# Strided attention on one core: another order of the first four loads

## The chip, the cores and the metric

The kernel runs on one core of a Trainium2 chip. The metric is the device time of one execution in microseconds (us), taken as the median of several runs; lower is better. Beside the times there is one execution recorded by the hardware profiler, with a trace of every instruction on the five engines (PE, the matrix engine; DVE, the vector engine; ACT, the scalar engine; POOL, the general engine; SP, which here only issues transfers) and of every packet that the 16 DMA engines moved.

## What is computed

Attention in which every query attends to only every 64th key, so 16 keys and 16 values for each of the 8 x 12 = 96 pairs of batch and head. The reference, cut to its core:

```python
# Q, K, V: float32, (batch, heads, seq, dim) = (8, 12, 1024, 64), stride = 64
for i in range(seq):
    attend_positions = np.arange(0, seq, stride)
    q = Q[:, :, i:i + 1, :]
    k = K[:, :, attend_positions, :]
    v = V[:, :, attend_positions, :]
    scores = np.einsum('bhqd,bhkd->bhqk', q, k) / np.sqrt(dim)
    weights = np.exp(scores - np.max(scores, axis=-1, keepdims=True))
    weights = weights / (np.sum(weights, axis=-1, keepdims=True) + 1e-10)
    result[:, :, i, :] = np.einsum('bhqk,bhkd->bhqd', weights, v)[:, :, 0, :]
```

Q is 25.17 MB, the result is as large, and the rows of K and V that are used are 0.39 MB each.

## The kernel before

**Tiling.** The 96 heads are cut into 24 groups of four (`NG = 24`, `HG = 4`). One group's queries are a block of 1 MiB (1.05 MB) that lands in one buffer `qn` as 128 partitions x 2048 floats. There are 18 such buffers (`BUFS = 18`), held two by two in the tiles `pair0` to `pair8`; a group's output is written back into the buffer that held its queries, and two groups are stored to HBM by one transfer of 2 MiB (the last two groups by one of 1 MiB each).

**Stages of a group.** `cast` turns the block to bf16 (tile `qb`; POOL alone at line 305, for the first three groups half on ACT at line 299 and half on POOL at line 301), `transpose` on DVE (`qt`, line 316), the products with the keys on PE (`sc`, line 324), the maximum and its subtraction on DVE (`top`, `low`), the exponential on ACT (`ex`, line 346), sum and reciprocal on DVE (`total`, `rec`), the multiplication on POOL (`wt_all`, line 358), a transpose on PE (`tp`), its spreading on ACT (`wb_all`, line 377), the products with the values on PE (`o`, line 385), and `evict` on ACT (line 403), which copies `o` into the query buffer. Then SP issues the store.

**Keys and values.** `load_rows` (line 235) fetches the 1536 used rows of K, and likewise of V, each row 256 bytes. `key_rows` casts the keys on ACT (line 263) and transposes them on DVE (line 264); `keys` (line 273) copies them into `k_t`, four copies on DVE for the even groups and four on ACT for the odd ones. `values` (line 287) places the values in `v_all`: eight small casts on POOL at once, the rest later on ACT and POOL.

**What sets the order.** Each engine has its instructions in the order in which the program was written out; an instruction that waits holds up everything behind it on its engine. On ACT this order begins: cast of the keys, half of query block 0, four copies of keys, half of query block 1, first exponential. On POOL: half of query block 0, the eight value casts, half of query block 1, half of query block 2, first `wt_all`. On DVE: transpose of the keys, four copies of keys, transpose of block 0.

All transfers are issued by SP on one hardware queue, from `_copy` (line 34, queries and outputs) or `load_rows` (line 236, keys and values), and each has its own semaphore. SP issues the first 20 loads back to back without waiting (K, query block 0, V, query blocks 1 to 17). From then on `queue` (line 454) sets its order: after every second group a store, and after the stores of groups 2-3, 4-5 and 6-7 two more query loads each (blocks 18 to 23). Block 18 goes into the buffer of group 0, block 19 into that of group 1, and so on, and SP waits until the store from that buffer has landed before it issues the load.

Of the kernel before, what the change touches and what calls it, by code (L numbers as in the profile page):

```python
# [18 lines left out]
def _ap_with(ap: bass.AP, new_ap, extra_offset: int = 0) -> bass.AP:  # L19
    return dataclasses.replace(  # L20
        ap, ap=[list(p) for p in new_ap], offset=ap.offset + extra_offset
    )


def _copy(nc, out: bass.AP, in_: bass.AP):

    sides = [
        mybir.BassSymbolicTensorAccessPattern(
            ap=side.ap, dtype=side.dtype, bass_ap=side,
            is_dma=True, for_custom_bir_dma=True,  # L30
        )
        for side in (in_, out)
    ]
    return nc.sync.add_instruction(  # L34
        mybir.InstDMACopy(
            name=nc.get_next_instruction_name(), engine=mybir.EngineType.SP,
            ins=sides[:1], outs=sides[1:], queue="qSPDynamicHW",
            mode="Copy",
        )
    )  # L40


class Program:
# [13 lines left out]
    def op(self, engine, fn, reads=(), writes=(), after=(), lane=None, gate=None, gates=(), times=1, looped=False, last=False):  # L57
        i = len(self.ops)
        deps, own = set(after), set()
        for k in reads:  # L60
            deps.add(self.writer.get(k))
            own.add(self.writer.get(k))
        for k in writes:
            deps.update(self.readers.get(k, ()))
            deps.add(self.writer.get(k))
            own.add(self.writer.get(k))
        deps.discard(None)
        for k in reads:
            self.readers.setdefault(k, []).append(i)
        for k in writes:  # L70
            self.writer[k], self.readers[k] = i, []
        self.ops.append(dict(
            engine=engine, fn=fn, lane=lane or engine, deps=deps, own=own,
            gate=gate, gates=gates, times=times, last=last, looped=looped,
        ))
        return i
# [92 lines left out]
def kernel(  # L169
# [21 lines left out]
    BUFS = 18  # L191
# [34 lines left out]
    def load(g):  # L226
        n = 32
        op("SP", lambda: _copy(
            nc, qn[g % BUFS],
            _ap_with(Q, [[HG * SD // n, n], [1, HG * SD // n]], g * HG * SD),  # L230
        ), writes=[f"qn{g % BUFS}{h}" for h in range(2)], lane=f"q{g % BUFS}")
# [3 lines left out]
    def load_rows(name, tile_, src, lane):  # L235
        op("SP", lambda: nc.sync.dma_start(tile_, _ap_with(src, kv_src)),
           writes=[name], lane=lane)

    load_rows("k_raw", k_raw, K, "k")
    load(0)  # L240
    load_rows("v_raw", v_raw, V, "v")
    for g in range(1, BUFS):
        load(g)

    op("POOL", lambda: nc.gpsimd.memset(identity, 0.0), writes=["identity"])
# [309 lines left out]
```

## Time and profile before

| | us |
|---|---|
| median of 3 runs | 128.17 |
| lowest and highest of them | 127.93 and 128.45 |
| the profiled execution, its own time | 127.63 |
| its span, first to last instruction | 125.8 |
| ACT busy in the span | 93.8 (75%) |
| DVE busy | 87.1 (69%) |
| POOL busy | 75.9 (60%) |
| PE busy | 58.1 (46%) |
| DMA queue busy, mean of 16 engines | 96.8% |

Read it from both ends. The shares of the compute engines are means over the span, and none of them works in the last fifth of it, so the shares say little of a single stage. The share of the DMA queue counts all 16 DMA engines. The page also draws the span as a line of 40 slices for each engine, a digit being the busy share in tenths; the time at the ends of these lines is what the argument below starts from. In tables by stretches of time, a packet's bytes are booked in the stretch in which it starts, so in short stretches the DMA share can be over 1.

### The profile page before, as it was taken

What the parts mean: (1) busy time and instruction counts of PE and PEld (TensorE: products, weight loads), DVE (VectorE), ACT (ScalarE), POOL (GpSimd) and SP (SyncE); (2) the same over time, 40 slices, a digit from 0 to 9 for tenths busy, and PEclk for the clock granted to TensorE, in tenths of its full rate; (3) what the DMA queues carried; (4) which work ended last, traced back from release to release, by engine and by line L of the source; (5) the groups of instructions that cost most, each with busy time, mean ns of one, the idle gap of its engine ahead of it and who ended that gap; (6) DMA issues with size and microseconds to landing.
All of it is one profiled execution on the core that took longest, in us unless ns stands there. A gap on an engine that the chain in (4) does not pass through costs nothing.

```text
span 125.8 us, 2084 instructions
## 1 busy us (share of the span) xinstructions
PE 58.1 (46%) x736; PEld 43.5 (35%) x736; DVE 87.1 (69%) x131; ACT 93.8 (75%) x109; POOL 75.9 (60%) x67
## 2 busy tenths in 40 slices
PE   0007672556489466665555565666656533000000
PEld 0006452445366444443443344444434321000000
DVE  3795879999979899999999999999966100000000
ACT  4266756999888999999999999999999965000000
POOL 5648589999998688889888888879233300000000
PEclk9999999998555999999999999999999975555555
DMA  1998989989899998999999999999999999999991
GB/s 41 425 406 385 490 365 479 448 385 479 365 479 437 406 469 354 422 422 479 417 391 458 422 385 432 464 406 424 417 422 422 427 427 437 427 432 417 406 424 65
DMA packets 6132, 51.15 MB, mean 406 GB/s; under 512 B 3696, under 2 KB 3696, under 8 KB 3696
## 3 DMA queue, kind: packets, MB, share of 16 engines
q1 hardware_dynamic: 6128, 51.12, 96.8%
q14 instruction: 4, 0.03, 0.1%
HBM read 25.95 MB, written 25.17 MB: 406 GB/s over the span
## 4 chain that ended last, share of the span: by engine, by line
ACT 51%; POOL 15%; DVE 7%; DMA 5%; PE 4%; issue 1%; SPq 1%; POOLq 0%
ACT pair L403 28%; ACT wb_all L377 16%; ACT ex L346 7%; POOL qb L305 6%; DMA v_raw<-in_V_dram 5%; POOL wt_all L358 4%; PE o L385 4%; POOL v_all L287 4%; DVE qt L316 3%; DVE total L351 1%; DVE top L338 1%; DVE rec L354 1%; POOL qb L301 1%; SPq L34 1%; DVE low L341 1%
## 5 line engine op out<-in xcount | busy, mean ns | idle before, releaser
L403 ACT COPY pair<-o 128x2048 f32<-128x2048 f32 x24 | 47.9, 1995 | 2.8 <-PE o L385 2.8
L305 POOL CAST qb<-pair 128x2048 bf16<-128x2048 f32 x21 | 39.7, 1892 | 1.5 <-DMA pair<-in_Q_dram 1.5
L385 PE MATMUL o<-v_all,wb_all 128*128 (+1 forms) x216 | 31.6, 295 | 8.2 <-ACT pair L403 8.2
L358 POOL TENSOR_TENSOR wt_all<-ex,rec 128x512 bf16<-128x512 f32 x24 | 25.4, 1058 | 15.4 <-DVE rec L354 15.1
L377 ACT ACTIVATE wb_all<-tp,sel 128x512 bf16<-128x512 bf16 x48 | 33.3, 810 | 0.7 <-PE tp L365 0.6
L316 DVE STREAM_TRANSPOSE qt<-qb 128x1024 int32<-128x1024 int32 x24 | 29.8, 1242 | 1.2 <-POOL qb L305 0.7
L385 PEld LDWEIGHTS o<-v_all,wb_all 128*128 128x128 bf16 x216 | 20.7, 105 | 14.9 <-issue 9.6
L324 PE MATMUL sc<-k_t,qt 128*128 x416 | 19.4, 200 | 12.9 <-DVE qt L316 12.8
L324 PEld LDWEIGHTS sc<-k_t,qt 128*128 128x128 bf16 x416 | 16.9, 103 | 17.5 <-issue 16.6
L365 PE MATMUL tp<-identity,wt_all 128*128 128x128 bf16 x104 | 11.1, 235 | 25.5 <-POOL wt_all L358 25.5
L346 ACT ACTIVATE ex<-low 128x512 f32<-128x512 f32 x24 | 18.3, 764 | 2.5 <-DVE low L341 2.5
L351 DVE TENSOR_REDUCE total<-ex 128x32 f32<-128x512 f32 x24 | 16.3, 678 | 3.9 <-ACT ex L346 3.9
L341 DVE TENSOR_TENSOR low<-sc,top 128x512 f32<-128x512 f32 x24 | 16.6, 691 | 0.8
L365 PEld LDWEIGHTS tp<-identity,wt_all 128*128 128x128 bf16 x104 | 6.4, 103 | 28.3 <-POOL wt_all L358 28.2
L338 DVE TENSOR_REDUCE top<-sc 128x32 f32<-128x512 f32 x24 | 15.2, 632 | 1.3 <-PE sc L324 1.3
L354 DVE RECIPROCAL rec<-total 128x32 f32<-128x32 f32 x24 | 8.5, 353 | 0.8
L287 POOL CAST v_all<-v_raw 32x128 bf16<-32x128 f32 (+1 forms) x12 | 5.2, 431 | 1.5 <-DMA v_raw<-in_V_dram 0.8
L299 ACT CAST qb<-pair 128x1024 bf16<-128x1024 f32 x3 | 3.1, 1045 | 3.1 <-DMA pair<-in_Q_dram 3.1
L301 POOL CAST qb<-pair 128x1024 bf16<-128x1024 f32 x3 | 3.1, 1039 | 3.3 <-DMA pair<-in_Q_dram 3.3
L259 POOL MEMSET v_all<- 128x3456 f32 x1 | 3.0, 2979 | 0.0
L287 ACT CAST v_all<-v_raw 32x640 bf16<-32x640 f32 x4 | 2.9, 722 | 0.0
L250 DVE MEMSET k_t<- 128x1664 uint32 x1 | 1.4, 1445 | 1.9 <-issue 1.9
(15 smaller groups left out, 9.6 us busy)
## 6 DMA issues: line engine op xcount, KB each, us to landing
pair<-in_Q_dram SPq DMA_DIRECT2D x24, 1024.0 KB, 15.0
out_dram<-pair SPq DMA_DIRECT2D x11, 2048.0 KB, 22.8
out_dram<-pair SPq DMA_DIRECT2D x2, 1024.0 KB, 18.7
k_raw<-in_K_dram SPq DMA_DIRECT2D x1, 384.0 KB, 3.9
v_raw<-in_V_dram SPq DMA_DIRECT2D x1, 384.0 KB, 6.8
```

Source lines behind the costliest of these rows:

```text
L305: op("POOL", lambda: nc.gpsimd.tensor_copy(out=b, in_=q), reads=[f"qn{g % BUFS}{h}" for h in range(2)] + apart, writes=[f"qb{g % 2}{h}" fo ...
L316: op("DVE", lambda: nc.vector.transpose(_ap_with(words, [words.ap[0], [1, 2], [D, 16], [2, 32]]), qb[g % 2].bitcast(I32),), reads=[f"qb{g ...
L324: r = nc.tensor.matmul(sc_ps[g % 2][:, 64 * i : 64 * i + 64], lhsT=_ap_with(qt[g % 2], [qt[g % 2].ap[0], [2, P]], extra_offset=2 * P * i + f),
L338: op("DVE", lambda: nc.vector.tensor_reduce(out=m, in_=s, op=ALU.max, axis=mybir.AxisListType.X,), reads=[f"sc{g % 2}"], writes=[f"top{g % ...
L341: op("DVE", lambda: nc.vector.tensor_tensor(out=low, in0=s, in1=m.unsqueeze(2).to_broadcast([P, 32, NK]), op=ALU.subtract,), reads=[f"sc{g ...
L346: op("ACT", lambda: nc.scalar.activation(out=ex[g % 2], in_=low, func=AF.Exp, bias=0.0, scale=scale,), reads=["low"], writes=[f"ex{g % 2}"])
L351: op("DVE", lambda: nc.vector.tensor_reduce(out=total[g % 2], in_=ex[g % 2], op=ALU.add, axis=mybir.AxisListType.X,), reads=[f"ex{g % 2}"] ...
L358: op("POOL", lambda: nc.gpsimd.tensor_tensor(out=wt[g % 2], in0=ex[g % 2], in1=rec[g % 2].unsqueeze(2).to_broadcast([P, 32, NK]), op=ALU.mult,
L365: r = nc.tensor.transpose(tp_ps[g % 2][:, 2 * c : 2 * c + 2].rearrange("p a b -> p (a b)"), wt[g % 2][:, 8 * c : 8 * c + 8].rearrange("p t ...
L377: op("ACT", lambda a=a: nc.scalar.activation(out=wb[g % 2][:, :, 64 * a : 64 * a + 64], in_=tp_ps[g % 2], func=AF.Copy, scale=sel[:, a : a ...
L385: r = nc.tensor.matmul(_ap_with(o_ps, [o_ps.ap[0], [128, 2], [256, 2], [1, D]], extra_offset=512 * c + D * u,), lhsT=wb[g % 2][:, 2 * c + ...
L403: op("ACT", lambda: nc.scalar.copy(to, o_ps.rearrange("p c (b x) -> p c b x", b=2)), reads=["o"], writes=[f"qn{g % BUFS}{n}" for n in rang ...
```

## The change

The first four loads are issued in another order: query block 0, K, query block 1, V, where it was K, query block 0, V, query block 1. Query blocks 2 to 17 follow as before. No instruction is added or removed, no size or wait of any engine is edited, and apart from these four transfers each engine has its instructions in the order it had.

```diff
@@ -236,10 +236,11 @@
         op("SP", lambda: nc.sync.dma_start(tile_, _ap_with(src, kv_src)),
            writes=[name], lane=lane)
 
+    load(0)
     load_rows("k_raw", k_raw, K, "k")
-    load(0)
+    load(1)
     load_rows("v_raw", v_raw, V, "v")
-    for g in range(1, BUFS):
+    for g in range(2, BUFS):
         load(g)
```

The place is the head of SP's stream. `pair0` is the tile that holds the buffers of query blocks 0 and 1, so both of its rows read alike; the first of them is block 0. Before:

```order
L236 DMA k_raw_71<-in_K_dram 128x12x64
L34 DMA pair0_62<-in_Q_dram 128x2048
L236 DMA v_raw_74<-in_V_dram 128x12x64
L34 DMA pair0_62<-in_Q_dram 128x2048
L34 DMA pair1_63<-in_Q_dram 128x2048 x2
```

After the change, the same place on SP:

```order
L34 DMA pair0_62<-in_Q_dram 128x2048
L236 DMA k_raw_71<-in_K_dram 128x12x64
L34 DMA pair0_62<-in_Q_dram 128x2048
L236 DMA v_raw_74<-in_V_dram 128x12x64
L34 DMA pair1_63<-in_Q_dram 128x2048 x2
```

K and V have each moved one place back, and each has now one query block more ahead of it in the queue; block 2 (the first of `pair1_63`) is where it was.

The engine that meets both of the moved loads early is POOL. With the change its stream reads as follows, row for row what it was (only the line numbers are one higher); `at_q0`, `at_q1`, `at_q2` and `at_v` are the semaphores of the loads of the query blocks 0 to 2 and of V:

```order
L302 CAST qb0_75<-pair0_62 128x1024 [waits at_q0]
L288 CAST v_all_82<-v_raw_74 32x2x64 [waits at_v,at_POOL]
L288 CAST v_all_82<-v_raw_74 32x2x64 [waits at_POOL] x7
L302 CAST qb1_76<-pair0_62 128x1024 [waits at_q1,at_POOL]
L144 UNCONDITIONAL_BRANCH
L302 CAST qb0_75<-pair1_63 128x1024 [waits at_q2,at_DVE,at_POOL]
```

Nothing moved here: the cast of block 1 still stands behind the eight casts of the values, although block 1 is now loaded ahead of them.

## The prediction

> **What bounds the kernel now.** I read the slices of the page first, then the end of the chain of waits, then the transfers.
>
> ```profile
> span 125.8 us, 2084 instructions
> DVE  3795879999979899999999999999966100000000
> ACT  4266756999888999999999999999999965000000
> DMA  1998989989899998999999999999999999999991
> 104.83 1.87 ACT pair L403
> 107.28 0.54 SPq L34 DMA_DIRECT2D out_dram<-pair  x1
> ```
>
> A slice is 3.1 us. The chain of waits ends with ACT's last eviction, at 104.83 + 1.87 = 106.7 us, and names ACT as half of the span; but that is where instructions end. The DMA line is full from the second slice to the last but one. The last store is issued at 107.28 us and the span runs 18.5 us longer, for a transfer of 1 MiB. How much was still queued is told by a table of stretches (columns: stretch, its length, busy time and count for PE, PEld, DVE, ACT, POOL, clock, DMA share, GB/s):
>
> ```profile
> 0.00:55.39 55.39, 29.03 (x359) 22.23 (x360) 47.59 (x69) 44.50 (x55) 44.85 (x45) 0.91 0.97 403
> 55.39:60.72 5.33, 3.45 (x52) 2.60 (x49) 5.19 (x10) 5.33 (x8) 4.23 (x4) 1.00 1.06 443
> 60.72:70.42 9.70, 5.98 (x84) 4.58 (x84) 9.53 (x15) 9.70 (x13) 8.14 (x6) 1.00 1.02 432
> 70.42:107.30 36.88, 19.66 (x245) 14.13 (x244) 24.80 (x41) 34.25 (x38) 18.71 (x14) 0.94 0.99 422
> 107.30:124.50 17.20, 0.00 (x0) 0.00 (x0) 0.00 (x0) 0.00 (x0) 0.00 (x0) 0.50 0.93 392
> ```
>
> After ACT's end the queue still moves 17.20 us x 392 GB/s = 6.7 MB; at the 422 GB/s of the row above that is 16 us of work, of which the last store itself is 1.05 MB or 2.5 us. So the store that ACT gates last came 13 us before the queue would have run dry. **The bound is the DMA queue**, from about 2 us to the end; no compute engine sets the end, busy as ACT is.
>
> One point in the middle could break this: SP waits for a landed store before it issues block 18.
>
> ```profile
> 29.60 0.63 SPq L34 DMA_DIRECT2D out_dram<-pair  x1
> 37.87 0.56 SPq L34 DMA_DIRECT2D out_dram<-pair  x1
> 55.39 1.30 SPq L34 DMA_DIRECT2D pair<-in_Q_dram  x2
> ```
>
> Issued by 55.39 us: 18 blocks of 1.049 MB, K and V of 0.393 MB each and two stores of 2.097 MB, 23.86 MB. Begun by then, by the first row of the table: 55.39 x 403 = 22.32 MB. So 1.54 MB, 3.6 us of work, was left, and the next row shows 443 GB/s: no gap.
>
> **The change, part by part.** It moves four transfers at the queue's head; nothing is added or removed. What counts is how early the queue gets to full rate, and whether the later keys and values make anything late that the queue waits for.
>
> The head of the queue before (the first three rows are SP's issues, the last four the table by stretches):
>
> ```profile
> 0.96 0.43 SPq L236 DMA_DIRECT2D k_raw<-in_K_dram  x1
> 1.45 0.74 SPq L34 DMA_DIRECT2D pair<-in_Q_dram  x1
> 2.24 0.82 SPq L236 DMA_DIRECT2D v_raw<-in_V_dram  x1
> 1.00:1.75 0.75, 0.00 (x0) 0.00 (x0) 0.00 (x0) 0.43 (x1) 0.20 (x1) 1.00 0.00 0
> 1.75:4.00 2.25, 0.00 (x0) 0.00 (x0) 1.93 (x2) 0.85 (x1) 2.16 (x2) 1.00 0.72 158
> 6.25:6.75 0.50, 0.00 (x0) 0.00 (x0) 0.45 (x3) 0.00 (x0) 0.00 (x0) 1.00 0.28 60
> 6.75:7.75 1.00, 0.00 (x0) 0.00 (x0) 0.97 (x3) 0.46 (x1) 0.43 (x1) 1.00 1.11 253
> ```
>
> *K in second place.* K has the queue from 1.75 to about 4.0 us: 2.25 us x 158 GB/s = 0.36 of its 0.39 MB, DMA share 0.72. V is the same shape, but comes behind a query block, and once under way it runs at 253 GB/s; 0.393 MB at that rate is 1.55 us. The difference, 2.25 - 1.55 = 0.70 us, is K's slow start on an empty queue. Behind a block, K's start lies beside that block's transfer, as V's does (issued at 2.24 us, moving from about 6.25 us). Term: -0.70 us. The stretch 6.25:6.75 at 60 GB/s, in which engines finish packets booked earlier and V sets in, is a turn from a block to rows; there are two such turns after the change and one before, but K's start then replaces a worse one, and I count none.
>
> *Query block 0 in first place.* What a block does on an empty queue the trace does not show. K's first packet comes 1.75 - 0.96 = 0.79 us after its issue begins, 0.36 us after its issue of 0.43 us ends. A block's issue takes 0.74 us. If the first packet follows the beginning of the issue, block 0 starts at 1.75 us as K did: 0. If it follows the end, it starts 0.74 - 0.43 = 0.31 us later: +0.31. If it has K's slow start as well, +0.31 + 0.70 = +1.01. I take +0.31: SP's issue is the only thing that the rows show ahead of the packets, and a block is few large packets, while K is 1536 rows of 256 bytes.
>
> The Trainium skill has a figure for this: DMA: Bandwidth & Descriptors, section Specifications, gives a first byte some 0.6 us after a load issued by SP. No run here shows a block on an empty queue; K's 0.79 us is somewhat longer. By the page block 0 would start at 1.56 us, 0.19 us ahead of K, and the sum would be an estimated -0.89 us.
>
> The same page speaks against the change (section Why small descriptors are slow): pieces of 256 bytes are slow because of a cost per piece, wherever they stand. By that alone K costs in second place what it cost in first, the first term is 0 and the sum +0.31 us. The trace agrees in part: V's 253 GB/s is well under 422, but K's 158 is lower still for the same pieces.
>
> *The consumers.* No cost on the queue, but the beginning of the compute is later, and this must be followed to the end:
>
> ```profile
> 4.86 0.83 ACT L263 CAST k_half<-k_raw 128x768 bf16<-128x768 f32 x1 [2.26 <-DMA k_raw<-in_K_dram]
> 7.29 1.04 ACT L299 CAST qb<-pair 128x1024 bf16<-128x1024 f32 x1 [1.60 <-DMA pair<-in_Q_dram]
> 8.71 1.25 DVE L316 STREAM_TRANSPOSE qt<-qb 128x1024 int32<-128x1024 int32 x1
> 9.13 2.75 POOL L287 CAST v_all<-v_raw 32x128 bf16<-32x128 f32 x8 [0.77 <-DMA v_raw<-in_V_dram]
> 11.47 1.04 ACT L299 CAST qb<-pair 128x1024 bf16<-128x1024 f32 x1 [1.04 <-DMA pair<-in_Q_dram]
> ```
>
> K and block 0 together are in by 7.29 us; with K second, the keys' cast starts there (less the 0.4 us won) instead of at 4.86: 2.4 us later. Behind it on ACT waits its half of block 0, long landed; on DVE the keys' transpose and four copies, then the transpose of block 0, at about 8.71 + 2.4 = 11.1 us. V and block 1 together are in by 11.47; with V second, POOL's eight value casts start at about 11.5 instead of 9.13, again 2.4 us later, and the cast of block 1 stands behind them although its data is there. Both arms are late by the same 2.4 us (2.0 with the gain), so the first exponential, the first `wt_all` and all behind them are. From about 40 us on ACT's slices above are full, so it cannot catch up. So the first store is issued at about 31.6 to 32.0 us, the second at about 40, and the last at about 109.5.
>
> Does the queue notice? The first two stores lie behind query blocks that occupy the queue until about 48 us (19.66 MB of loads at 422, from 2 us on), so they are still 8 us early. The wait at 55.39 is for the first of them to land, which the queue sets, not ACT. At the end, 13 us of queued work cover 2.4. Cost: 0; without that cover it would be the whole 2.4 us. The loads that compute waited for later are only less urgent.
>
> *Sum:* -0.70 + 0.31 = -0.39 us, 127.63 - 0.39 = 127.24 us for the profiled execution. That execution is 0.54 us under the median of the runs shown (its own share outside the span is 127.63 - 125.8 = 1.83 us, which I leave), so against the median 128.17 - 0.39 = 127.8 us. Bounds: best -0.70 (no cost for block 0), worst +0.31 (slow start kept by whatever is first: -0.70 + 1.01).
>
> The end adds its own uncertainty:
>
> ```profile
> 122.00:122.75 0.75, 0.00 (x0) 0.00 (x0) 0.00 (x0) 0.00 (x0) 0.00 (x0) 0.50 1.01 426
> 122.75:123.50 0.75, 0.00 (x0) 0.00 (x0) 0.00 (x0) 0.00 (x0) 0.00 (x0) 0.50 0.45 186
> 123.50:124.50 1.00, 0.00 (x0) 0.00 (x0) 0.00 (x0) 0.00 (x0) 0.00 (x0) 0.50 0.12 49
> ```
>
> The 16 engines do not finish together: from 122.75 to 124.5 us they move 0.14 + 0.05 = 0.19 MB, 0.45 us of work spread over 1.75 us. Another order at the head can change which engine is last; I allow 0.5 us either way.
>
> **The rivals.** *A deeper gain:* block 0 fills the queue at once and K's start vanishes whole: -0.70, with an even end -0.9, 127.3 us. For it speaks that a block is large packets; against it the longer issue. *Slower, the late keys reach the end:* place, the stores; price, the 2.4 us above, 130.6 us. It decides from the point at which the queue runs dry before a store is issued: at the end if ACT were over 13 us late, or at 55.39 us if the 3.6 us of queued work fell under the 0.8 us that a new load takes to its first packet. Both margins are larger than 2.4 us, and the second isn't ACT's to shorten; I see little for it. *The order does not matter:* whatever stands first pays the slow start, +0.31 at most, about 128.3 us; for it, that the trace shows only one transfer on an empty queue.
>
> **How the numbers follow.** What a measurement of this kernel can tell from no change is about 0.5%, 0.64 us: faster is under 127.53, slower over 128.81. The forecast has 0.50, the deeper gain 0.25, no matter 0.17, the late keys 0.08. Faster: the deeper gain and a tenth of the forecast (its own spread passes 127.53 on that side), 0.30. Slower: the late keys, and 0.03 from the case of no matter with an uneven end, 0.11. Same: 0.59. Range: 128.17 - 0.70 - 0.5 = 127.0 to 128.17 + 0.31 + 0.4 = 128.9; outside it lie the late keys and a little more.
>
> **What would show it.** Right: the DMA line still full to the last but one slice, with 0.4 us less at its end; K's cast at about 7 us and POOL's value casts at about 11; the first store at about 32 us and the last at about 109.5, yet the load of block 18 still issued at about 55. The stretch table would show the full rate soon after 2.1 us and K's 0.39 MB inside some 1.6 us. Wrong: a hole in the DMA line behind 48 us, or the last store less than 5 us ahead of the end (then the late keys decide); a slow first 2 us with block 0 (then the order does not matter).

## The result and the profile after

| | us |
|---|---|
| before, median of 20 runs | 128.12 (127.86 to 128.72) |
| changed, median of 20 runs | 128.39 (128.06 to 129.08) |
| ratio | 1.0026, 95% interval 1.0016 to 1.0035 |
| the profiled execution of the changed kernel, its own time | 128.46, span 126.7 |

The change costs 0.27 us by the medians (0.33 us by the ratio) where 0.39 us of gain was forecast. It is under the 0.5% that the prediction counts as a change, but its sign is clear, and it came again in two other sessions (1.0027 and 1.0024, below). The time lies in the stated range; the forecast's sign was wrong. A run more than 1.5% above the fastest of its kernel is left out of every ratio in this document: four of ten of opener_half (130.30 to 131.99 us) and one of the kernel before.

The profile after, lines that answer to those shown of before: the slices and the end of the chain of waits, then SP's issues.

```profile
span 126.7 us, 2084 instructions
ACT  4039374799989999999999999999999993400000
DMA  2899999999999999999999989999999999999991
107.17 1.87 ACT pair L404
```

```profile
0.95 0.58 SPq L34 DMA_DIRECT2D pair<-in_Q_dram  x1
1.60 0.56 SPq L236 DMA_DIRECT2D k_raw<-in_K_dram  x1
32.43 0.62 SPq L34 DMA_DIRECT2D out_dram<-pair  x1
55.97 1.17 SPq L34 DMA_DIRECT2D pair<-in_Q_dram  x2
109.61 0.54 SPq L34 DMA_DIRECT2D out_dram<-pair  x1
```

The DMA line is full to the last slice but one, as before. ACT ends at 109.0 instead of 106.7 us and the last store is issued 2.3 us later, yet the span grew by 0.9 us only. The consumers are late, and by more than was reckoned: the keys' cast starts at 8.29 us where about 7 was said, the value casts at 12.19 where 11 to 11.5 was said. In the timelines of ACT and POOL:

```profile
8.29 0.83 ACT L264 CAST k_half<-k_raw 128x768 bf16<-128x768 f32 x1 [5.70 <-DMA k_raw<-in_K_dram]
12.19 2.74 POOL L288 CAST v_all<-v_raw 32x128 bf16<-32x128 f32 x8 [4.72 <-DMA v_raw<-in_V_dram]
```

The difference to look at is in the first microseconds of the queue. The table by stretches (columns as in the prediction), of the changed kernel:

```profile
1.75:2.25 0.50, 0.00 (x0) 0.00 (x0) 0.35 (x1) 0.50 (x1) 0.41 (x2) 1.00 0.19 49
2.25:3.00 0.75, 0.00 (x0) 0.00 (x0) 0.75 (x1) 0.34 (x1) 0.75 (x1) 1.00 0.00 0
3.00:3.50 0.50, 0.00 (x0) 0.00 (x0) 0.44 (x2) 0.00 (x0) 0.50 (x1) 1.00 2.58 1049
```

and of the kernel before, the same stretches:

```profile
1.75:2.25 0.50, 0.00 (x0) 0.00 (x0) 0.35 (x1) 0.50 (x1) 0.41 (x2) 1.00 0.19 45
2.25:3.00 0.75, 0.00 (x0) 0.00 (x0) 0.75 (x1) 0.35 (x1) 0.75 (x1) 1.00 0.44 96
3.00:3.50 0.50, 0.00 (x0) 0.00 (x0) 0.44 (x2) 0.00 (x0) 0.50 (x1) 1.00 1.23 253
```

The 49 GB/s of the first row are 24.5 KB, three packets of 8 KB, and they are instructions: this line of the page counts them apart from the transfers.

```profile
q14 instruction: 4, 0.03, 0.1%
```

So in this execution no byte of block 0 moves before 3.0 us, 2.06 us after its issue began, while K's rows move from 2.08 us, 1.12 us after theirs. The prediction took the instruction packets at 1.75 us for K's first.

### The profile page after: what moved, and what is told of

Read it like the earlier page. It is cut to its first block, busy times and chain, and to the rows that moved or that the text cites. A ratio compares the mean times of both kernels' runs of the same rounds, so it can differ in the third digit from the quotient of the medians.

```text
span 126.7 us, 2084 instructions
## 1 busy us (share of the span) xinstructions
PE 57.2 (45%) x736; PEld 42.9 (34%) x736; DVE 86.2 (68%) x131; ACT 93.5 (74%) x109; POOL 75.8 (60%) x67
## 4 chain that ended last, share of the span: by engine, by line
ACT 53%; POOL 16%; DMA 7%; PE 4%; issue 4%; SPq 2%; POOLq 0%
ACT pair L404 29%; ACT wb_all L378 16%; ACT ex L347 8%; DMA v_raw<-in_V_dram 7%; POOL qb L306 6%; POOL wt_all L359 4%; PE o L386 4%; POOL v_all L288 4%; POOL qb L302 2%; SPq L34 1%; PE tp L366 0%; SPq L236 0%; POOLq L157 0%; SPq L551 0%; SPq L142 0%
## 5 line engine op out<-in xcount | busy, mean ns | idle before, releaser
L404 ACT COPY pair<-o 128x2048 f32<-128x2048 f32 x24 | 48.6, 2024 | 2.5 <-PE o L386 2.4
L386 PE MATMUL o<-v_all,wb_all 128*128 (+1 forms) x216 | 31.1, 292 | 8.5 <-ACT pair L404 8.5
L378 ACT ACTIVATE wb_all<-tp,sel 128x512 bf16<-128x512 bf16 x48 | 34.0, 840 | 0.5 <-PE tp L366 0.5
L347 ACT ACTIVATE ex<-low 128x512 f32<-128x512 f32 x24 | 19.0, 790 | 5.4 <-DVE low L342 5.4
L264 ACT CAST k_half<-k_raw 128x768 bf16<-128x768 f32 x1 | 0.8, 831 | 5.7 <-DMA k_raw<-in_K_dram 5.7
L265 DVE STREAM_TRANSPOSE k_half<-k_half 128x384 int32<-128x384 int32 x1 | 0.6, 578 | 4.1 <-ACT k_half L264 4.1
```

The lines of the kernel that those rows point to most:

```text
L347: op("ACT", lambda: nc.scalar.activation(out=ex[g % 2], in_=low, func=AF.Exp, bias=0.0, scale=scale,), reads=["low"], writes=[f"ex{g % 2}"])
L378: op("ACT", lambda a=a: nc.scalar.activation(out=wb[g % 2][:, :, 64 * a : 64 * a + 64], in_=tp_ps[g % 2], func=AF.Copy, scale=sel[:, a : a ...
L386: r = nc.tensor.matmul(_ap_with(o_ps, [o_ps.ap[0], [128, 2], [256, 2], [1, D]], extra_offset=512 * c + D * u,), lhsT=wb[g % 2][:, 2 * c + ...
L404: op("ACT", lambda: nc.scalar.copy(to, o_ps.rearrange("p c (b x) -> p c b x", b=2)), reads=["o"], writes=[f"qn{g % BUFS}{n}" for n in rang ...
```

## The experiments

Sixteen runs beside the two at hand, in five sessions, each with its own runs of the kernel before. All ratios are to those. One table from the packet records of the traces serves them all; it was worked out by sorting a trace's packets by their end. "Block 2 starts" is the mean over the 16 DMA engines of the first packet of query block 2, the first transfer whose place in the queue is the same in all versions of the table; "40 MB" is when 40 MB had been moved.

```
version            first   0.4 MB  0.8 MB  block 2  40 MB   last     ratio to before
                   packet  moved   moved   starts   moved   packet
before              2.08    5.27    5.54    10.57    97.64  124.60   1
before_again        2.08    5.43    5.84    10.78    97.93  125.13   1.0000
swap_values         2.07    5.30    5.72    10.59    97.80  124.99   1.0003
keys_block_rows     2.07    4.72    5.74    10.91    98.01  125.21   1.0006
block_rows          1.98    4.13    5.11    10.76    97.82  124.87   0.9997
block_rows_again    1.97    4.09    5.06    10.77    97.83  125.36   0.9994
block_8k            2.33    4.19    5.17    10.88    97.90  124.84   1.0020
block_16k           2.32    4.49    5.39    11.19    98.16  125.43   1.0013
changed             3.02    4.60    5.82    11.30    98.36  125.43   1.0026
after_again         2.33    4.46    5.68    10.81    98.03  125.30   1.0027
after_third         2.35    4.61    5.76    11.06    98.15  125.02   1.0024
rows_first          2.08    4.24    6.86    10.92    99.00  126.04   1.0040
opener              2.04    5.05    6.28    11.52    98.56  126.20   1.0064
opener_half         2.08    4.90    6.12    11.45    98.94  125.98   1.0050
swap_keys           2.33    4.58    5.74    11.26    99.44  126.68   1.0101
swap_keys_again     2.31    4.50    5.74    11.58    99.17  125.55   1.0088
```

One trace is one execution, and executions of one kernel differ: block 2 starts at 10.57 and 10.78 us in two of the kernel before, at 11.30, 10.81 and 11.06 us in three of the changed one. The means, 10.68 and 11.06, differ by 0.38 us; at 40 MB, 97.79 and 98.18, it is 0.39 us. In the eleven rows above rows_first, the time from block 2's start to the 40 MB is 86.97 to 87.22 us, so what is lost at the head is still lost at 40 MB, to within 0.25 us.

**before_again and after_again**: both kernels unedited. The first asks why the two traces at hand differ by 0.83 us and the medians by 0.27.

> The kernel before, unedited, profiled once more. The two profiled executions at hand differ by 0.83 us (127.63 and 128.46) while the medians of 20 runs each differ by 0.27 us (128.12 and 128.39). First theory (the time is set by when the queue's first packet moves, 2.08 us here against 3.02 us with the change): another execution whose time lies near 128.1 has its first packet later than 2.08 us, at about 2.4 to 2.6, and from block 2 on the queue runs as before. Rival (the end decides): first packet at 2.08 us again, and the missing half microsecond lies at the end, where the 16 engines finish unevenly. Ratio 1.000 by either.

> The changed kernel, unedited, profiled once more. First theory: first packet about 2 us after its issue begins, at 3.0 us, and block 2 begins 0.7 us later than in the first trace of the kernel before; ratio about 1.002 to 1.003. Rival (the time comes from the late compute): the first packet varies freely and the time does not follow it.

before_again: 1.0000 (0.9987 to 1.0012), its profiled execution 128.16 us, with the first packet at 2.08 us again: the first theory's guess of a later first packet fell. Of the 0.53 us by which this execution is longer, 0.21 are there at block 2, and 0.24 come at the end, where the last packet ends 125.13 - 97.93 = 27.20 us after the 40 MB instead of 26.96. The first trace of the kernel before was a short one at both ends. after_again: 1.0027 (1.0011 to 1.0043), with the first packet at 2.33 us, not 3.0. The time did not follow it: the packets that began early took longer, and at 0.4 MB the three traces of the changed kernel lie within 0.15 us.

**swap_keys and swap_values**: each half of the change alone.

```diff
+    load(0)
     load_rows("k_raw", k_raw, K, "k")
-    load(0)
     load_rows("v_raw", v_raw, V, "v")
```

is swap_keys, and swap_values is

```diff
     load_rows("k_raw", k_raw, K, "k")
     load(0)
+    load(1)
     load_rows("v_raw", v_raw, V, "v")
-    for g in range(1, BUFS):
+    for g in range(2, BUFS):
```

> Only K and block 0 change places: block 0, K, V, block 1. First theory (a block in first place has its first packet 0.9 us later, K behind it saves 0.2): the whole of the change's cost is here, ratio 1.002 to 1.006, block 2 begins 0.7 us later than in the first trace of the kernel before. Rival (each turn from a block to rows costs queue time, and the change has one such turn more): with K and V side by side there is one turn as before, so the ratio is 1.000 or below. Rival (V behind block 1 is what costs, through POOL's value casts): ratio 1.000.

> Only V and block 1 change places: K, block 0, block 1, V. First theory: first packet as before, block 2 begins as before within 0.1 us, ratio 1.000 within 0.001, although POOL's value casts start at about 11.5 us and the first store is issued about 2 us later. Rival (late compute reaches the end): slower by as much as the changed kernel is, 1.002 to 1.003, or by the whole 2.4 us (1.019).

swap_values: 1.0003 (0.9993 to 1.0013). Its timelines of POOL and SP:

```profile
11.37 2.74 POOL L288 CAST v_all<-v_raw 32x128 bf16<-32x128 f32 x8 [2.81 <-DMA v_raw<-in_V_dram]
31.60 8.81 SPq L34 DMA_DIRECT2D out_dram<-pair  x2
```

The value casts start 2.2 us later and the first store is issued 2.0 us later, and the time stays. Late compute of that size costs nothing that is seen here, and V's move by itself is not the cause. swap_keys: 1.0101 (1.0074 to 1.0128), four times the whole change; no theory had asked for that. Block 2 starts 0.6 us later than the mean of before, about as in the changed kernel, and something is lost again at 49 us. Around it, by stretches, swap_keys:

```profile
49.00:50.00 1.00, 1.00 (x13) 0.91 (x14) 1.00 (x2) 1.00 (x3) 1.00 (x1) 1.00 1.77 426
50.00:51.00 1.00, 0.50 (x17) 0.37 (x13) 0.97 (x3) 1.00 (x2) 0.45 (x2) 1.00 0.04 16
```

Almost no packet starts between 50 and 51 us: the 16 packets begun before take 1.9 to 2.4 us each instead of 1.2.

**swap_keys_again and rows_first**: is the stall of this order, and does it need K and V side by side? rows_first loads K, V, block 0, block 1.

```diff
     load_rows("k_raw", k_raw, K, "k")
-    load(0)
     load_rows("v_raw", v_raw, V, "v")
-    for g in range(1, BUFS):
+    load(0)
+    load(1)
+    for g in range(2, BUFS):
```

> Block 0, K, V, block 1 once more. The first run came out at 1.0101, 0.7% more than the changed kernel, and its trace holds a stall of all 16 engines by about 1 us each at 49.5 us, where the last of the first loads is moved, beside a head that ends as late as in the changed kernel's first trace. Theory (the stall belongs to this order and comes in every execution): ratio 1.008 to 1.012 and the stall at 49 to 50 us again. Rival (a disturbance of that session): ratio 1.002 to 1.004 and no stall.

> K and V both ahead of block 0: K, V, block 0, block 1. First theory (what opens the queue decides, and K opens it soonest): first packet at 2.08 us, block 2 within 0.2 us of the kernel before, ratio 0.999 to 1.002, though block 0 and so all compute comes 1.5 us later. Rival (each turn between rows and blocks costs): one turn less than before, ratio 0.997 or less. Rival (two row transfers side by side bring the stall of the swapped keys): ratio 1.008 or more.

swap_keys_again: 1.0088 (1.0067 to 1.0109), rows_first: 1.0040 (1.0023 to 1.0057), which is between what its first theory and the rival of the stall had said. Packets that took over 0.15 us longer than their size usually takes, begun between 46 and 51.5 us, their excess summed and divided by 16 engines: 1.16 us (26 packets) and 0.45 us (23) in the two traces of swap_keys, 1.10 us (31) in rows_first, at most 0.07 us (5) in every other trace. These are the three traced executions with K and V next to each other. So the stall belongs to that order, though in differing amounts; how the order brings it about is open. Both kernels under study keep a block between K and V and have none of it.

**block_8k and block_16k**: the changed order with block 0 in smaller pieces, from the same line 34.

```diff
-    def load(g):
-        n = 32
+    def load(g, n=32):
...
-    load(0)
+    load(0, 128)      # block_16k: 64
```

> The changed order, with block 0 alone cut into 128 rows of 8 KB instead of 32 of 32 KB. In the two traces of the changed kernel block 0 is through (mean end of its packets) 4.1 to 4.2 us after its issue begins, of which 2.4 us are transfer: 1.7 us late, where K's first packet comes at 1.1 us. First theory (the lateness belongs to the large pieces: an engine moves nothing of a 32 KB packet until all of it is described and its first read is back): with 8 KB pieces block 0 is through 0.3 to 0.6 us earlier, and the ratio falls from 1.0027 to 0.998 to 1.000. Rival (the lateness belongs to whichever block opens the queue, whatever its pieces): ratio 1.002 to 1.004 as before, first packet 1.4 to 2.1 us after the issue begins. Rival (more pieces, later start): ratio over 1.005.

> As the run before, with 64 rows of 16 KB for block 0. If piece size decides, it lies between 8 KB and 32 KB, ratio about 1.000 to 1.002. If the opening of the queue decides, 1.002 to 1.004.

1.0020 (1.0009 to 1.0031) and 1.0013 (1.0000 to 1.0027). The 8 KB pieces are through earlier at first (0.8 MB at 5.17 us instead of 5.68 to 5.82), but the time hardly gains: against 1.0026 the intervals overlap. The size of the pieces is not shown to matter, and by the 1.0013 it could account for up to half of the cost; the theory's 0.998 to 1.000 was missed.

**block_rows, twice, and keys_block_rows**: block 0 issued in K's way, as 128 rows of 8 KB, first in the queue (block_rows) and behind K as before (keys_block_rows). The edit of block_rows, against the kernel before:

```diff
+    op("SP", lambda: nc.sync.dma_start(
+        qn[0], _ap_with(Q, [[2048, P], [1, 2048]]),
+    ), writes=["qn00", "qn01"], lane="q0")
     load_rows("k_raw", k_raw, K, "k")
-    load(0)
+    load(1)
     load_rows("v_raw", v_raw, V, "v")
-    for g in range(1, BUFS):
+    for g in range(2, BUFS):
```

> The changed order, with block 0 issued in the way that K is (by the line of load_rows, as 128 rows of 8 KB) instead of by the copy of line 34. Theory (a block opens the queue slowly in whatever way it is issued): first packet 1.4 us or more after its issue begins, ratio 1.001 to 1.003, as with 8 KB pieces. Rival (the way of issuing makes K's start early): first packet 1.1 us after, ratio 0.998 to 1.000.

> The changed order with block 0 issued in the way of K's load, once more, beside the changed kernel on the same chip. Theory A (block 0's lead is shorter by the 0.2 to 0.35 us that its issue and first packet come sooner): 0.9990 to 1.0010, and below the changed kernel by 0.0015 to 0.004. Rival (the first run was chance): 1.002 to 1.003, as the 8 KB pieces from line 34 gave.

> The changed kernel once more, for the comparison with the run before. 1.002 to 1.003; first packet at 2.3 us as in the second trace, or at 3.0 us as in the first; in either case block 0's first packets are through at 4.4 to 4.5 us on average, 3.4 to 3.6 us after its issue begins.

> The order before (K first), with block 0 issued in the way of K's load, as 128 rows of 8 KB. If what that way of issuing saved in the changed order (0.3%) is a quicker opening of the queue, it saves nothing here, where K opens the queue and covers block 0's lead: ratio 0.999 to 1.001. If it is a cheaper transfer wherever it stands (smaller pieces at the turn from rows to a block), it saves here too: 0.995 to 0.998, a version faster than both.

block_rows: 0.9997 (0.9983 to 1.0010) and 0.9994 (0.9982 to 1.0006), with the changed kernel at 1.0024 (1.0015 to 1.0033) on the chip of the second: the whole cost of the change is gone, by another way of issuing its first load; the rival had said so, and the theory was missed. The pieces of 8 KB alone, issued from line 34 (block_8k), had left it at 1.0020. SP's first issue in block_rows, and the stretches of its head:

```profile
0.96 0.39 SPq L239 DMA_DIRECT2D pair<-in_Q_dram  x1
```

```profile
1.75:2.25 0.50, 0.00 (x0) 0.00 (x0) 0.35 (x1) 0.50 (x1) 0.41 (x2) 1.00 0.95 115
2.25:3.00 0.75, 0.00 (x0) 0.00 (x0) 0.75 (x1) 0.35 (x1) 0.75 (x1) 1.00 0.42 109
3.00:3.50 0.50, 0.00 (x0) 0.00 (x0) 0.45 (x2) 0.00 (x0) 0.50 (x1) 1.00 0.79 311
```

The issue takes 0.39 instead of 0.58 us and the first packet comes at 1.98 instead of 2.33 us or later. keys_block_rows, the same transfer behind K: 1.0006 (0.9995 to 1.0018), no gain. So what was won is the opening of the queue and not a cheaper transfer; in single traces it is small (block 2 starts at 10.76 and 10.77 us in block_rows, at 10.88 in block_8k), so its size is told by the ratios alone. And no version was faster than the kernel before.

**opener and opener_half**: the changed order with a sixth, or half, of K ahead of block 0. The main lines, against the changed kernel:

```diff
+    load_keys("k_raw0", slice(0, 2))      # opener_half: slice(0, 6)
     load(0)
-    load_rows("k_raw", k_raw, K, "k")
+    load_keys("k_raw1", slice(2, NC))     # opener_half: slice(6, NC)
     load(1)
```

> The changed order with a sixth of K ahead of it: 256 rows of K, block 0, the other 1280 rows of K, block 1, V. Theory (a block needs some 2.2 us from its issue until it moves at full rate; rows begin at 1.1 us, and in the kernel before K's rows fill just that time): the first packet comes at 2.08 us, block 0 moves from about 3.0 us, and the ratio is 1.000 to 1.001, although K is complete as late as in the changed kernel and all compute 2 us late. Rival (rows in second place are what costs): ratio 1.002 to 1.004 as in the changed kernel. Rival (one transfer more costs by itself): over 1.004.

> As the opener run, with half of K (768 rows) ahead of block 0 and the other half behind it. Theory A (every transfer moves at full rate only some 2.2 us after its own issue begins; block 0, issued at 1.45 us, is ready at about 3.7 us, and rows that move until then cost nothing): 768 rows, at about 1000 a microsecond once under way, last until about 3.5 us, only 0.2 us stays empty instead of about 1.0 us with 256 rows, and the ratio falls from 1.0064 to 1.001 to 1.003. Theory B (the queue as a whole opens at about 3 us, whatever has been issued; splitting K costs by itself): ratio 1.005 to 1.008 as with 256 rows.

1.0064 (1.0046 to 1.0082) and 1.0050 (1.0035 to 1.0065): both expectations of the theory were missed. The rival that one transfer more costs by itself had said over 1.004 for opener; no run here tells that cost from a later start of block 0. In opener, block 0 is issued at 1.45 us instead of 0.96, and its first packets are through at 4.99 us on average, instead of 4.38 to 4.51 in the changed kernel: that is later by about the 0.49 us by which its issue moved, so rows ahead of it did not hide its slow opening. With half of K ahead they are through at 5.20 us and block 2 starts as late (11.45 us): more rows ahead bought nothing. That a transfer's lead, the time from its issue to full rate, runs from its own issue fits opener. But opener_half was to tell this from a queue that opens late as a whole, and by the number given ahead it speaks for the latter; this stays open.

**values_after_4 and values_after_8**: K first as before, V only behind block 4 or block 8, to find how late compute may be.

```diff
     load_rows("k_raw", k_raw, K, "k")
-    load(0)
+    for g in range(5):                    # values_after_8: range(9)
+        load(g)
     load_rows("v_raw", v_raw, V, "v")
-    for g in range(1, BUFS):
+    for g in range(5, BUFS):              # values_after_8: range(9, BUFS)
```

> K first as before, V only after block 4: K, blocks 0 to 4, V. POOL's value casts, and all compute behind them, come 4 blocks or 9.7 us later; the last store is issued at about 117 us. Theory (13 us of queued work cover late compute at the end): ratio 0.999 to 1.002. Rival (late compute reaches the end, in whole or in part): 1.01 to 1.076.

> V only after block 8: compute 8 blocks or 19.4 us later, more than the 13 us of cover. The last eviction ends at about 126 us, and one store of 1 MiB needs some 5 us from issue to the end of the span: span about 131 to 132 us against 126.2. Theory: ratio 1.035 to 1.055, and a DMA line with holes at the end. Rival (the cover is larger than reckoned, or compute catches up): under 1.02.

values_after_4: 1.0029 (1.0014 to 1.0043). The first store is issued at 38.90 us, 9.3 us late, and the time rises by 0.4 us, a little more than the theory allowed. The queue has moved 40 MB at 97.95 us, as before. The last packet ends 27.59 us later, which is within the 26.38 to 27.64 us of the table's versions, so one trace does not show where the 0.4 us lie. values_after_8: 1.042 (1.0369 to 1.0472), inside what was expected, but the hole is not where it was expected. SP's issues, with ACT's eviction of the fourth group between them, and the stretches of the queue's hole:

```profile
48.71 8.82 SPq L34 DMA_DIRECT2D out_dram<-pair  x2
54.55 1.87 ACT pair L404
57.57 1.96 SPq L34 DMA_DIRECT2D pair<-in_Q_dram  x2
```

```profile
54.00:56.00 2.00, 1.41 (x20) 1.12 (x19) 1.93 (x3) 1.56 (x2) 1.88 (x3) 0.50 0.31 131
56.00:58.00 2.00, 1.88 (x23) 1.34 (x24) 0.99 (x3) 2.00 (x5) 1.74 (x1) 0.96 0.00 0
```

The first loads are through at 49.8 us, and from then on the first store, issued at 48.71 us, is alone in the queue; its last packet ends at 55.03 us. The second store needs the eviction that ends at 56.42 us and comes at 57 us; block 18 stands behind it on SP, although its buffer has been free since the first store landed. From 55 to 58 us nothing moves. So the queue runs dry in the middle, while SP waits for compute at the second store, before the cover at the end is used up.

## Why the prediction was wrong

**The bound: right.** The DMA queue sets the time from its first packet to its last. The 0.38 us between the means at block 2 is still 0.39 us at 40 MB, and swap_values, 2 us late in its compute, is as fast as the kernel before.

**"Term: -0.70 us", K in second place: right in size, in part by luck.** The stretch was read as 1.75 to about 4.0 us. Its beginning was that of the instruction packets, 0.33 us before K's first, and its end was 0.24 us too early as well, so that the length came out nearly right. In the kernel before K holds an engine from its first packet at 2.08 us to the mean start of block 0 at 4.24 and 4.45 us in two traces: 2.27 us on average. Behind block 0, from that block's end to block 1's start, it is 1.67, 1.38 and 1.50 us in the three traces of the changed kernel: 1.52. The difference is 0.75 us. The Trainium skill (DMA: Bandwidth & Descriptors, section Why small descriptors are slow) lays the slowness on a fixed cost of each piece. Behind a block, 1.52 us for 0.39 MB is still more than the 0.93 us that 422 GB/s would need, so it holds there; the further 0.75 us in first place is not of the pieces.

**"I take +0.31", block 0 in first place: this is the step that failed.** Block 0's first packets are through at 4.51, 4.38 and 4.50 us in the three traces of the changed kernel; less the 1.21 us that a packet takes, it is as if the block moved at full rate from 3.25 us on, 1.17 us behind K's first packet. What the term counted, a later first packet, did come about as reckoned: in two of the three traces the first packet is at 2.33 and 2.35 us, some 0.26 us behind K's, though the issue took 0.58 to 0.59 us and not 0.74. In those two the first packets took up to 2.1 us instead of 1.2; in the third the first packet itself came at 3.02 us. What it left out is that slow start. The prediction had the right case among its three, "K's slow start as well", +1.01 us, and put it aside because a block is few large packets. No row of the trace before showed a large packet starting faster; the only transfer seen on an empty queue had a slow start, and that was the nearest row. With what the runs showed the sum is -0.75 + 1.17 = +0.42 us, beside 0.38 us between the traces' means and some 0.3 us by the ratios (1.0024 to 1.0027). So the slow start that was to be removed is paid by the block that now opens the queue; the rival "the order does not matter" had said so, with 128.3 us, and the median is 128.39.

That the opening is the cause is shown by one pair: the other way of issuing block 0 takes away the change's cost where the block opens the queue (0.9997 and 0.9994 against 1.0024), and nothing where K does (1.0006). Why a block reaches its full rate only some 2.3 us after its issue begins is not shown.

**The first byte after some 0.6 us** that the Trainium skill gives (same page, section Specifications) would have made an estimated gain of 0.89 us, counted from the beginning of the issue. The first packet came 1.0 to 1.4 us after that in all traces but one, and 2.06 us in that one; the estimate fell. Counted from the end of the issue it is 0.62 to 0.80 us in all but that one (1.49 us), so the figure nearly fits the first packet, though not the time to full rate, on which the sum depends.

**The consumers' cost of 0: right** as far as swap_values shows it, for 2 us. The stores are about as late as reckoned (first store 32.43 us where 31.6 to 32.0 was said, last store 109.61 where about 109.5 was said), though the casts ahead of them are later. Of the two margins given, 8 us at the first two stores and 13 us at the end, the rival of the late keys named the end and block 18's load: values_after_8 shows that the second store, with block 18 behind it, gives way first.

**The spread at the end** was allowed 0.5 us, and it is there: between 40 MB and the last packet lie 26.96 and 27.20 us in two traces of before. The head spreads as much: 0.73 of the 0.83 us between the first two traces are there at block 2, where the means differ by 0.38.

## What to carry to other kernels

Where a transfer queue is full to the end, only its opening and its holes count. Follow a change in load order to the point at which the queue first moves at full rate. Count late compute as free until the queue would run dry, and look for that point at the stores in the middle as well as at the end. A slow start seen on the first transfer may be the price of being first, as here; then moving that transfer back hands the price to its successor, so assume that unless a trace shows the successor starting quicker. And one profiled execution can lie 0.5 us off its median: differences of that size need the medians, and several traces for their place.

## What the runs showed of the hardware that was not expected

The way of issuing the first load is worth 0.2 to 0.3% by the ratios (0.9997 and 0.9994 against 1.0020, in different sessions): an issue of 0.39 us with the first packet 1.0 us after it began (block_rows), against 0.58 us and 1.4 us for pieces of the same 8 KB from the other line (block_8k).

Two transfers of 256-byte rows next to each other in the queue are followed, some 40 us later, by a stall of 0.45 to 1.16 us as a mean over the 16 engines (swap_keys twice, rows_first), which no trace with a block between them shows. What connects the two was not found.
